# Stick-breaking attention on one core: the running products recorded one step later

## The chip, the core and the metric

The kernel runs on one core of a Trainium2 chip. The metric is the device time of one execution in microseconds (us), the median of several runs of the same program. TensorE (PE in the profile) multiplies matrices, with its weight loads in a row of their own (PEld); VectorE (DVE), ScalarE (ACT) and GpSimd (POOL) work on tiles; SyncE's queue (SP) issues most of the transfers. Each engine takes its instructions in one fixed order, and an instruction starts when the semaphores that it names have come.

## What is computed

A two-layer encoder over 2048 positions of 1024 channels. Layer 0 is a gated pooling mixer, layer 1 is strictly causal stick-breaking attention with 16 heads of 64 channels; each layer ends with a residual and a gated embedding add. The change touches layer 1 alone:

```
q, z = split(rms_norm(x) @ b_w_in);  q = rms_norm(q)       # k, v: once, shared
A[t,s] = beta[t,s] * prod_{s<j<t} (1 - beta[t,j]),  beta = sigmoid(q.k / sqrt(d))
x = x + ((A @ v) * silu(z)) @ b_w_out
x = x + (p[1] @ ple_w[1]) * sigmoid(x @ ple_gate_w[1])
```

The kernel works with the running product of 1 - beta from the newest key backwards. A position's weight is the difference of two neighbouring running products, so the kernel multiplies the products themselves with a v whose rows were differenced beforehand.

## The kernel before

A first part (0 to about 1330 us of the span) computes layer 0 and q, k and v for all four chunks of 512 positions, and stores them. The second part is attention, with the dense work of layer 1 spread between its steps.

**Slots and steps.** A slot is one chunk c of queries, one head h and one chunk kc of keys, from c = 3 down to 0 and within a head from the diagonal chunk (kc = c) back to 0. There are 160 slots. A slot takes four steps, one for each 128 queries (j) and later one for each 128 keys (kt): 640 steps, in the loop at line 1167. One step n does, in the order in which the code is written:

- `turn` (line 943) for the slot that began six steps earlier: up to four 128x128 transposes of running products into a PSUM tile `psa` (L949, PE), the high part of it by a cast (L952, ACT), and the low part by a subtraction on VectorE (L953), called the split here; both go to the tile `at`. There are two `psa` buffers, so the transposes of a step wait for the split two steps earlier.
- `front` (line 917) for the present slot: two matmuls into `psl` (L924, L925, PE), and the sigmoid into one of four tiles `kap` (L928, ACT). It hands back `scan`, the running product on VectorE (L933 on a diagonal slot, L936 elsewhere), which reads `kap` and writes `pp`.
- `scan()`, called at once (line 1184).
- the filler: some passes of dense matmuls from a generator (line 1188; L994, L996 and L998 in `piecewise`). Behind every 24 passes, or 6, a result in PSUM is taken out on VectorE. These three are called the drains here: L1028 in `gate_z` (zr = psd * rb, followed by a sigmoid on ACT, L1032, and a product on POOL, L1033), L1058 in `post` (xr = psd + xr), and L1086 in `post` (sg = psd * sg, followed by an add on POOL, L1087, and one on VectorE, L1088). Each of the four `gate_z` begins with a tile of scales `rb`, of which there is one: four transposes into a `psa` buffer (L1020) and a copy on ACT (L1022), which has to wait until the last L1028 has read the old `rb`.
- `settle` for work put off by some steps, and `gather` (line 956) for the slot that began eight steps earlier: two matmuls of `vv` with `at` (L961, L962, PE).

`shares` (line 1125) sets how many filler passes each step gets while the first chunk of queries runs, out of estimated times of VectorE and TensorE in that step; later the passes are spread evenly.

**What sets the order.** The code's order is a priority. A list scheduler places the instructions engine by engine by its own estimate of when each is ready: an instruction written later goes first where the earlier one is not ready. Instructions marked as kept in program order are not moved. So the order that counts is that of the built program, which is shown in the section on the change. In its rows the running product is named SCALAR_TENSOR_TENSOR, where the profile says TENSOR_TENSOR_SCAN.

Of the kernel before, what the change touches and what calls it, by code (L numbers as in the profile page):

```python
# [35 lines left out]
def trunk_kernel(ctx, tc, x, xt, pt0, wut, cols, heads, zin, grp, aout, agate, aple,  # L36
# [182 lines left out]
    with ExitStack() as st:  # L219
# [41 lines left out]
        def settle():  # L261
            while late:
                late.pop(0)()
# [592 lines left out]
    with ExitStack() as st:  # L856
# [60 lines left out]
        def front(st, j):  # L917

            w = (j + 1) * P if st["diag"] else W5
            r0 = W5 - w  # L920
            ps = psl.tile([P, W5], F32, tag="psl", name="psl")
            qs = slice(j * P, (j + 1) * P)
            (qa, qb), kk = st["q"], st["k"]
            T.matmul(ps[:, :w], qa[:, qs], kk[:, :w], start=True, stop=False)  # L924
            T.matmul(ps[:, :w], qb[:, qs], kk[:, :w], start=False, stop=True)  # L925
            kp = kaps[kcount[0] % NK]
            kcount[0] += 1
            A.activation(out=kp[:, r0:], in_=ps[:, :w], func=AF.Sigmoid, scale=-1.0)  # L928

            def scan():  # L930
                pp = ppool.tile([P, W5], F32, tag="pp", name="pp")
                if st["diag"]:
                    V.tensor_tensor_scan(out=pp[:, r0:][:, ::-1], data0=kp[:, r0:][:, ::-1],  # L933
                                         data1=ahead[:, r0:][:, ::-1], initial=1.0, op0=ALU.mult, op1=ALU.max)
                else:
                    V.tensor_tensor_scan(out=pp[:, ::-1], data0=kp[:, ::-1], data1=zeros.to_broadcast([P, W5]),  # L936
                                         initial=st["carry"][j], op0=ALU.mult, op1=ALU.add)
                st["carry"][j] = pp[:, r0 : r0 + 1]
                st["a"].append((pp, r0))

            return scan

        def turn(st, kt):

            j0 = kt if st["diag"] else 0
            pt = psa.tile([P, W5], F32, tag="psa", name="psa")
            for j in range(j0, 4):
                pp, r0 = st["a"][j]
                T.transpose(pt[:, j * P : (j + 1) * P], pp[:, r0 + kt * P : r0 + (kt + 1) * P], ident)  # L949
            at = t2.tile([P, 2, W5], F32R, tag="at", name="at", bufs=3)  # L950
            cs = slice(j0 * P, W5)
            A.copy(out=at[:, 0, cs], in_=pt[:, cs])  # L952
            V.tensor_tensor(out=at[:, 1, cs], in0=pt[:, cs], in1=f(at[:, 0, cs]), op=ALU.subtract)  # L953
            st["at"][kt] = at

        def gather(st, kt):
            cs = slice((kt if st["diag"] else 0) * P, W5)
            if st["diag"] and kt == 0:
                st["o"].append(pso.tile([P, W5], F32, tag="pso", name="pso"))
            po, at, vv = st["o"][0], st["at"].pop(kt), st["v"]  # L960
            T.matmul(po[:, cs], vv[:, kt, :], at[:, 0, cs], start=(st["diag"] and kt == 0), stop=False)  # L961
            T.matmul(po[:, cs], vv[:, kt, :], at[:, 1, cs], start=False, stop=(st["last"] and kt == 3))  # L962
            if st["last"] and kt == 3:
                half, os, ob, c, h2 = st["h"] % 2, st["os"], st["ob"], st["c"], st["h"] // 2
                mine, other = slice(half * HD, (half + 1) * HD), slice((1 - half) * HD, (2 - half) * HD)

                def gated():
                    zt = t2.tile([P, W5], F32, tag="zt", name="zt", bufs=1)
                    nc.sync.dma_start(out=zt, in_=zd[c][h2])
                    for j in range(4):  # L970
                        js = slice(j * P, (j + 1) * P)
                        stay(A.activation(out=os[:, js], in_=os[:, js], func=AF.Identity,  # L972
                                          bias=ends[c][:, h2, j : j + 1]))
                    G.tensor_tensor(out=os, in0=os, in1=zt, op=ALU.mult)  # L974

                soon(1, lambda: stay(A.copy(out=ob[mine], in_=po[other])))
                soon(2, lambda: stay(A.copy(out=os[mine], in_=po[mine])))
                if half:
                    soon(3, lambda: V.tensor_tensor(out=os, in0=os, in1=ob, op=ALU.add))
                    soon(4, gated)  # L980
                    soon(6, lambda: outs[c].append(os))
# [143 lines left out]
        def shares(n0, n1, total):  # L1125
            scan, turned_, gathered = ([widths(n, lag) for n in range(n0, n1)] for lag in (0, LAG_T, LAG_G))
            vector = [(0.15 + 0.0022 * a if a else 0.0) + (0.14 + 0.00105 * t if t else 0.0) for a, t in zip(scan, turned_)]
            tensor = [2 * max(0.109, 0.2265 * a / W5) * (a > 0) + 0.109 * t / P + 2 * max(0.109, 0.2265 * g / W5) * (g > 0)
                      for a, t, g in zip(scan, turned_, gathered)]
            part = lambda k: [max(0.5, (k * v - t) / 0.2265) + (AHEAD if n0 + i < LAG_T else 0)  # L1130
                              for i, (v, t) in enumerate(zip(vector, tensor))]
            lo, hi = 0.0, 20.0
            for _ in range(60):
                mid = (lo + hi) / 2
                lo, hi = (mid, hi) if sum(part(mid)) < total else (lo, mid)
            return dict(zip(range(n0, n1), part(hi)))
# [12 lines left out]
        for n, (c, _, _) in enumerate(slots):  # L1149
            stops[c] = 4 * (n + 1) + LAG_G + 6  # L1150
        share, even = shares(0, stops[NSUB - 1], NSUB * POSTZ - HELD), 0.0
        done = set()
        ends = {}

        def begin(i):
            c, h, kc = slots[i]
            if kc == c:
                if h == 1:
                    early["ends"] = load_ends(c)
                os = head["os"] if h % 2 else t2.tile([P, W5], F32, tag="os", name="os", bufs=9)  # L1160
                ob = head["ob"] if h % 2 else t2.tile([P, W5], F32, tag="ob", name="ob", bufs=1)
                head.clear()
                head.update(q=early.pop("q", None) or load_q(c, h), carry=[None] * 4, o=[], os=os, ob=ob)
            kk = early["k"].pop(0) if early["k"] else load_k(kc, h)
            active[i] = dict(head, c=c, h=h, k=kk, v=load_v(kc, h), diag=kc == c, last=kc == 0, a=[], at={})

        for n in range(4 * len(slots) + LAG_G):
            now[0] = n
            i2, j2 = divmod(n - LAG_T, 4)
            if 0 <= i2 < len(slots):  # L1170
                turn(active[i2], j2)
            i, j = divmod(n, 4)
            scan = None
            if i < len(slots):
                c, h, kc = slots[i]
                if j == 0:
                    if i == 0:
                        begin(0)
                    if i + 1 < len(slots):
                        begin(i + 1)  # L1180
                scan = front(active[i], j)
                if "ends" in early and j == 2:
                    early.pop("ends")()
            if scan is not None:
                scan()
            owed += even or share.get(n, 0.0)
            while owed >= 1.0:
                next(filler, None)
                owed -= 1.0
            if n >= 4 and n % 4 == 1 and early["s"]:  # L1190
                early["s"].pop(0)()
            if n >= LAG_G and n % 4 == 2 and early["v"]:
                early["v"].pop(0)()
            settle(n)
            i3, j3 = divmod(n - LAG_G, 4)
            if 0 <= i3 < len(slots):
                gather(active[i3], j3)
                if j3 == 3:
                    active.pop(i3)
            for c in range(NSUB - 1, 0, -1):  # L1200
                if len(outs[c]) == 8 and c not in done:
                    done.add(c)
                    for _ in filler:
                        settle()
                    filler = beside(c - 1)
                    if c == NSUB - 1:
                        share = shares(n + 1, stops[c - 1], POST + HELD)
                    else:
                        even = POST / (64.0 * c - (LAG_G + 2 if c == 1 else 1))
                    owed = 0.0  # L1210
# [56 lines left out]
```

## Time and profile before

| | |
|---|---|
| median of 3 runs | 2701.68 us (2701.57 to 2701.96) |
| the profiled execution's own time | 2702.68 us |
| its span, first to last instruction | 2700.8 us |
| DVE busy in the span | 1938.8 us, 72% |
| ACT busy in the span | 1399.2 us, 52% |
| POOL busy in the span | 923.9 us, 34% |
| DMA | 581.56 MB, 215 GB/s on average |

The profile counts an engine as busy from an instruction's start to its end; for PE the ends are modelled, since matmuls are pipelined. A wait is the idle time ahead of an instruction, put down to what ended last before it.

### The profile page before, as it was taken

Reading aid. Unit: us, or ns where it says so; the run is one execution under the profiler, and the core shown is the slowest. Engines: PE = TensorE matmul, PEld = TensorE weight load, DVE = VectorE, ACT = ScalarE, POOL = GpSimd, SP = SyncE. Lnnn points to the kernel's source line nnn. Section 1 sums busy time; section 2 is a strip of 40 time slices with the busy share of each in tenths; the row PEclk is TensorE's granted clock in tenths of the full one; section 3 lists DMA queues with packets and bytes.
Section 4 is the critical chain, followed back from the end, with each engine's and each line's share of the span. In section 5 each row is a group of like instructions: output and inputs, shape, how many; then the busy total and the mean of one; then the engine's idle time right before and its main releaser. Section 6 shows DMA issues by size and latency. Waiting matters only on the chain. (4 is left out here: it accounts for less than half of the span.)

```text
span 2700.8 us, 38620 instructions
## 1 busy us (share of the span) xinstructions
PE 2675.5 (99%) x13352; PEld 2226.3 (82%) x13352; DVE 1938.8 (72%) x2503; ACT 1399.2 (52%) x2735; POOL 923.9 (34%) x725
## 2 busy tenths in 40 slices
PE   9999999999999999999999999999999999999999
PEld 8888888888888888888878888888888888888877
DVE  6776625755367543755399999999999998986632
ACT  6445523455135541445366666666666666665530
POOL 2675338633485425753121111122111211222220
PEclk9999999999999999999999999999999999999999
DMA  8647785567856678444788665555655576668965
GB/s 327 222 169 281 250 302 191 203 228 254 299 173 232 241 243 292 144 150 163 220 237 282 191 209 173 163 169 179 192 161 169 178 215 202 189 199 261 268 220 171
DMA packets 276544, 581.56 MB, mean 215 GB/s; under 512 B 33110, under 2 KB 66902, under 8 KB 276348
## 3 DMA queue, kind: packets, MB, share of 16 engines
q1 hardware_dynamic: 270610, 571.41, 64.6%
q10 hardware_dynamic: 5738, 7.68, 1.0%
q8 instruction: 106, 1.74, 0.3%
q14 instruction: 90, 0.74, 0.1%
HBM read 438.40 MB, written 132.19 MB: 211 GB/s over the span
## 5 line engine op out<-in xcount | busy, mean ns | idle before, releaser
L952 ACT CAST at<-psa 128x512 fp32r<-128x512 f32 (+3 forms) x640 | 334.7, 523 | 436.5 <-PE psa L949 427.1
L614 PE MATMUL psd<-wpair,x 128*128 128x512 f32 x2304 | 536.9, 391 | 0.0
L936 DVE TENSOR_TENSOR_SCAN pp<-kap,pp,zeros 128x512 f32<-128x512 f32 x384 | 513.4, 1337 | 6.3 <-ACT kap L928 5.4
L614 PEld LDWEIGHTS psd<-wpair,x 128*128 128x128 f32 x2304 | 429.9, 188 | 87.1
L953 DVE TENSOR_TENSOR at<-psa,at 128x512 fp32r<-128x512 f32 (+3 forms) x640 | 381.4, 596 | 83.7 <-ACT at L952 78.7
L949 PE MATMUL psa<-ident,pp 128*128 128x128 f32 x2176 | 344.8, 274 | 13.3 <-DVE at L953 12.6
L928 ACT ACTIVATE kap<-psl 128x512 f32<-128x512 f32 (+3 forms) x640 | 345.2, 539 | 13.4 <-PE psl L925 10.5
L949 PEld LDWEIGHTS psa<-ident,pp 128*128 128x128 f32 x2176 | 265.2, 140 | 81.5 <-DVE at L953 26.1
L924 PE MATMUL psl<-kk,qa 128*128 128x512 f32 (+3 forms) x640 | 282.3, 441 | 0.3 <-DMA kk<-kd 0.3
L962 PE MATMUL pso<-at,vv 128*128 128x512 f32 (+3 forms) x640 | 234.4, 366 | 1.2 <-DVE at L953 1.2
L925 PE MATMUL psl<-kk,qb 128*128 128x512 f32 (+3 forms) x640 | 232.9, 364 | 0.0
L961 PE MATMUL pso<-at,vv 128*128 128x512 f32 (+3 forms) x640 | 232.8, 364 | 0.0
L933 DVE TENSOR_TENSOR_SCAN pp<-kap,ahead 128x128 f32<-128x128 f32 (+3 forms) x256 | 227.1, 887 | 5.2 <-ACT kap L928 3.2
L167 PE MATMUL psd<-xp,wpair 128*128 128x512 f32 x512 | 199.6, 390 | 1.4 <-DVE xp L316 1.4
L166 PE MATMUL psd<-xp,wpair 128*128 128x512 f32 x512 | 200.2, 392 | 0.2 <-ACT xp L315 0.2
L168 PE MATMUL psd<-xp,wpair 128*128 128x512 f32 x512 | 199.3, 390 | 0.0
L149 DVE SCALAR_TENSOR_TENSOR wpair<-wraw,gains,wpair 128x512 fp32r<-128x512 f32 x192 | 161.5, 882 | 48.7 <-ACT wpair L148 43.0
L143 POOL TENSOR_TENSOR wpair<-wraw,wpair 128x512 fp32r<-128x512 f32 x99 | 145.4, 1478 | 81.7 <-ACT wpair L141 80.5
L148 ACT ACTIVATE wpair<-wraw,gains 128x512 fp32r<-128x512 f32 x192 | 132.7, 718 | 71.2 <-DMA wraw<-in_bq_dram 32.6
L1033 POOL TENSOR_TENSOR zr<-zr,sgz 128x512 f32<-128x512 f32 x32 | 62.0, 1939 | 309.8 <-ACT sgz L1032 239.8
L141 ACT CAST wpair<-wraw 128x512 fp32r<-128x512 f32 x148 | 90.0, 618 | 121.8 <-PE psd L168 86.6
L962 PEld LDWEIGHTS pso<-at,vv 128*128 128x128 f32 x640 | 120.3, 188 | 27.8 <-DVE at L953 2.0
(196 smaller groups left out, 5364.3 us busy)
## 6 DMA issues: line engine op xcount, KB each, us to landing
kk<-kd SPq DMA_DIRECT2D x320, 128.0 KB
vv<-vd SPq DMA_DIRECT2D x160, 256.0 KB
wraw<-in_kv_dram SPq DMA_DIRECT2D x128, 256.0 KB
wpair<-wzd SPq DMA_DIRECT2D x64, 512.0 KB
wpair<-wod SPq DMA_DIRECT2D x64, 512.0 KB
wpair<-wgd SPq DMA_DIRECT2D x64, 512.0 KB
wpair<-wu SPq DMA_DIRECT2D x48, 512.0 KB
wpair<-wi SPq DMA_DIRECT2D x36, 512.0 KB
```

The source lines that it names most:

```text
L166: T.matmul(ps, wst(units, kt, 0, c0), acts[kt][:, 0], start=(begin and kt == order[0]), stop=False)
L614: T.matmul(pss2[i], ck["x2"][kt][:, xh, tk], wst(ws, kt, wh, 0, W5), start=(kt == 0 and xh == 0 and wh == 0), stop=(kt == KT - 1 and wh == 1))
L924: T.matmul(ps[:, :w], qa[:, qs], kk[:, :w], start=True, stop=False)
L925: T.matmul(ps[:, :w], qb[:, qs], kk[:, :w], start=False, stop=True)
L928: A.activation(out=kp[:, r0:], in_=ps[:, :w], func=AF.Sigmoid, scale=-1.0)
L933: V.tensor_tensor_scan(out=pp[:, r0:][:, ::-1], data0=kp[:, r0:][:, ::-1], data1=ahead[:, r0:][:, ::-1], initial=1.0, op0=ALU.mult, op1=AL ...
L936: V.tensor_tensor_scan(out=pp[:, ::-1], data0=kp[:, ::-1], data1=zeros.to_broadcast([P, W5]), initial=st["carry"][j], op0=ALU.mult, op1=AL ...
L949: T.transpose(pt[:, j * P : (j + 1) * P], pp[:, r0 + kt * P : r0 + (kt + 1) * P], ident)
L952: A.copy(out=at[:, 0, cs], in_=pt[:, cs])
L953: V.tensor_tensor(out=at[:, 1, cs], in0=pt[:, cs], in1=f(at[:, 0, cs]), op=ALU.subtract)
L961: T.matmul(po[:, cs], vv[:, kt, :], at[:, 0, cs], start=(st["diag"] and kt == 0), stop=False)
L962: T.matmul(po[:, cs], vv[:, kt, :], at[:, 1, cs], start=False, stop=(st["last"] and kt == 3))
```

## The change

The call of `scan` is put into a list, and is made at the beginning of the next step, ahead of that step's `turn`.

```
-        done = set()
+        done, behind = set(), []
...
         for n in range(4 * len(slots) + LAG_G):
             now[0] = n
+            if behind:
+                behind.pop()()
             i2, j2 = divmod(n - LAG_T, 4)
             if 0 <= i2 < len(slots):
                 turn(active[i2], j2)
...
             if scan is not None:
-                scan()
+                behind.append(scan)
             owed += even or share.get(n, 0.0)
```

As the code is written, step n's scan then stands behind step n's filler, `settle` and `gather`, and still between the split of step n and that of step n + 1. In the built program PE's order and POOL's are what they were. On VectorE scans and splits alternate as before; of the 96 drains (32 of each kind) 25 change places with the scan ahead of them: 15 L1028, 6 L1058 and 4 L1086. One L1088 goes ahead of a split, two copies L1022 on ACT go ahead of a cast L952, and one cast L1062 on ACT (the high part of a drained xr) ahead of a sigmoid. SP's queue has three changes, each a transfer moved past one neighbour.

The first place is one such swap on VectorE, at the last L1028 of the third `gate_z` (zr is the drained tile, kap and pp belong to the scan, at to the split). Before:

```order
L953 TENSOR_TENSOR at<-psa,at 128x512
L936 SCALAR_TENSOR_TENSOR pp<-kap_12445,pp,zeros 128x512
L953 TENSOR_TENSOR at<-psa,at 128x512
L936 SCALAR_TENSOR_TENSOR pp<-kap_12442,pp,zeros 128x512
L1028 TENSOR_TENSOR zr<-psd,rb 128x512
L953 TENSOR_TENSOR at<-psa,at 128x512
L936 SCALAR_TENSOR_TENSOR pp<-kap_12443,pp,zeros 128x512
```

And of the change, at the same place:

```order
L953 TENSOR_TENSOR at<-psa,at 128x512
L936 SCALAR_TENSOR_TENSOR pp<-kap_12445,pp,zeros 128x512
L953 TENSOR_TENSOR at<-psa,at 128x512
L1028 TENSOR_TENSOR zr<-psd,rb 128x512
L936 SCALAR_TENSOR_TENSOR pp<-kap_12442,pp,zeros 128x512
L953 TENSOR_TENSOR at<-psa,at 128x512
L936 SCALAR_TENSOR_TENSOR pp<-kap_12443,pp,zeros 128x512
```

The drain L1028 and the scan behind the second split have changed places; the splits around them have not moved.

The second place is on ACT, where the third `gate_z` fills `rb` out of `psar`. Before:

```order
L952 CAST at<-psa 128x512
L928 ACTIVATE kap_12444<-psl 128x512
L952 CAST at<-psa 128x512
L1022 COPY rb<-psar 128x512
L928 ACTIVATE kap_12445<-psl 128x512
L1032 ACTIVATE sgz<-zr 128x512
```

And of the change:

```order
L952 CAST at<-psa 128x512
L928 ACTIVATE kap_12444<-psl 128x512
L1022 COPY rb<-psar 128x512
L952 CAST at<-psa 128x512
L928 ACTIVATE kap_12445<-psl 128x512
L1032 ACTIVATE sgz<-zr 128x512
```

The copy L1022 stands one cast earlier. The L1028 that it waits for is one of the 25 that moved.

The third place is on VectorE at the end of the first `post`, with the last drain L1086 there and the add L1088 that waits for POOL's L1087. Before:

```order
L953 TENSOR_TENSOR at<-psa,at 128x512
L936 SCALAR_TENSOR_TENSOR pp<-kap_12443,pp,zeros 128x512
L1086 TENSOR_TENSOR sg<-psd,sg 128x512
L953 TENSOR_TENSOR at<-psa,at 128x512
L1088 TENSOR_TENSOR sg<-sg,x_20497 128x512
L936 SCALAR_TENSOR_TENSOR pp<-kap_12444,pp,zeros 128x512
L953 TENSOR_TENSOR at<-psa,at 128x384
```

And of the change:

```order
L953 TENSOR_TENSOR at<-psa,at 128x512
L1086 TENSOR_TENSOR sg<-psd,sg 128x512
L936 SCALAR_TENSOR_TENSOR pp<-kap_12443,pp,zeros 128x512
L1088 TENSOR_TENSOR sg<-sg,x_20495 128x512
L953 TENSOR_TENSOR at<-psa,at 128x512
L936 SCALAR_TENSOR_TENSOR pp<-kap_12444,pp,zeros 128x512
L953 TENSOR_TENSOR at<-psa,at 128x384
```

The drain L1086 goes ahead of a scan, and the add L1088 ahead of the split behind that scan.

More of the change, by code (lines that the diff above doesn't have):

```diff
@@ L1151, in trunk_kernel @@
         share, even = shares(0, stops[NSUB - 1], NSUB * POSTZ - HELD), 0.0
-        done = set()
+        done, behind = set(), []
         ends = {}
@@ L1168, in trunk_kernel @@
             now[0] = n
+            if behind:
+                behind.pop()()
             i2, j2 = divmod(n - LAG_T, 4)
@@ L1184, in trunk_kernel @@
             if scan is not None:
-                scan()
+                behind.append(scan)
             owed += even or share.get(n, 0.0)
```

## The prediction

> **What bounds the kernel now.** I read the page's table of engines first, then the waits of PE, then stretches of the attention.
>
> ```profile
> span 2700.8 us, 38620 instructions
> PE 2675.5 (99%) x13352; PEld 2226.3 (82%) x13352; DVE 1938.8 (72%) x2503; ACT 1399.2 (52%) x2735; POOL 923.9 (34%) x725
> ```
>
> PE is idle for 2700.8 - 2675.5 = 25.3 us of the whole span. Its order is not changed, so a change that only moves other engines' work can win back at most that, and can cost only by making PE wait.
>
> ```profile
> PE psa L949 <- DVE at L953: 12.6, 21, 1.5
> ...
> PE psl L924 <- DMA kk<-kd: 0.3, 1, 0.3
> ```
>
> ```profile
> DVE at L953 <- ACT at L952: 78.7, 153, 2.2
> ...
> DVE sg L1088 <- POOL sg L1087: 17.1, 12, 2.3
> ```
>
> These are waits, PE's first and then those of all engines: who waited for whom, us in total, how often, the longest. The first is the only place of weight where VectorE holds PE in the attention: the transposes L949 wait for the split L953 that frees their PSUM tile, 21 times in 640 steps. VectorE itself mostly waits for ACT's cast, which follows PE's transposes; so PE leads and VectorE follows.
>
> ```profile
> 1340.00:1900.00 560.00, 553.90 (x3048) 460.12 (x3047) 541.86 (x644) 360.92 (x723) 99.04 (x53) 1.00 0.65 200
> 1900.00:2200.00 300.00, 295.43 (x1642) 247.39 (x1641) 290.81 (x354) 196.59 (x408) 52.18 (x31) 1.00 0.57 177
> ```
>
> Two stretches of the attention: their length, then busy time of PE, PEld, DVE, ACT and POOL, the granted clock (1.00), and the transfers. VectorE is busy for 541.86 / 560 = 97% and 290.81 / 300 = 97%. So it has next to no reserve there: what lengthens its work step after step would soon reach PE. The question is whether a drain in another place does.
>
> **The change part by part.** Nothing is added or removed: 32 drains of each kind, 384 + 256 scans and 640 splits stay. Scans and splits alternate as before. What moves is 25 drains, each from behind a scan to ahead of it.
>
> ```profile
> L1028 DVE TENSOR_TENSOR zr<-psd,rb 128x512 f32<-128x512 f32 x32 | 21.4, 669 | 0.3
> L1086 DVE TENSOR_TENSOR sg<-psd,sg 128x512 f32<-128x512 f32 x24 | 16.2, 675 | 2.5 <-PE psd L998 1.9 <-ACT sg L1082 0.4
> L1058 DVE TENSOR_TENSOR xr<-psd,xr 128x512 f32<-128x512 f32 x24 | 16.2, 673 | 1.1 <-issue 0.8 <-PE psd L998 0.4
> ```
>
> ```profile
> L936 DVE TENSOR_TENSOR_SCAN pp<-kap,pp,zeros x384: 1266/1275/2335, 1341.7 to 2418.9; 128x512 f32<-128x512 f32 x192
> ```
>
> Groups of VectorE from 1340 to 2600 us (busy, mean ns, then idle before), and the scan's least, median and longest duration in ns. A drain takes 0.67 us and waits for nearly nothing; a scan takes 1.28. The ordinary swap is best seen at 1746 us, the first place in the section on the change:
>
> ```profile
> 1744.45 0.40 PE L998 MATMUL psd<-xz,wpair 128*128 128x512 f32 x1
> ...
> 1744.81 0.69 DVE L953 TENSOR_TENSOR at<-psa,at 128x512 fp32r<-128x512 f32 x1
> ...
> 1745.42 1.28 DVE L936 TENSOR_TENSOR_SCAN pp<-kap,pp,zeros 128x512 f32<-128x512 f32 x1
> ...
> 1746.61 0.67 DVE L1028 TENSOR_TENSOR zr<-psd,rb 128x512 f32<-128x512 f32 x1
> ...
> 1747.30 0.69 DVE L953 TENSOR_TENSOR at<-psa,at 128x512 fp32r<-128x512 f32 x1
> ```
>
> Start, duration, engine, line. The dense product ends at 1744.45 + 0.40 = 1744.85, the split at 1745.50. In its new place the drain finds its operand 0.65 us old and starts at once; the scan follows 0.6 us later; the next split starts at 1747.30 as before, since the sum of the two is the same. The drain ends 1.2 us earlier and frees a PSUM tile that PE doesn't ask for until a whole group of passes later, so nothing is gained. The scan ends 0.6 us later; its result is turned at the earliest three steps later, after two more splits and two more scans on VectorE, and its `kap` tile is written again four steps later. That hides it: **0 us**, for 22 of the 25. If VectorE were more than a step behind PE, the cover would be gone, and each would cost 0.6.
>
> In one of the 22 the drain would not start at once:
>
> ```profile
> 1403.48 0.69 DVE L953 TENSOR_TENSOR at<-psa,at 128x512 fp32r<-128x512 f32 x1 [0.23 <-ACT at L952]
> ...
> 1403.90 0.39 PE L998 MATMUL psd<-x,wpair 128*128 128x512 f32 x1
> ...
> 1404.49 1.28 DVE L936 TENSOR_TENSOR_SCAN pp<-kap,pp,zeros 128x512 f32<-128x512 f32 x1 [0.33 <-ACT kap L928]
> ```
>
> Its product ends at 1404.29 and the split at 1404.17, so it waits 0.12, inside the 0.33 that the scan waited for ACT anyway. This too is 0.
>
> SP's three swapped transfers are each a load or store by one neighbour: in the whole attention PE waited 0.3 us for a load of keys, and never longer for one; 0. So with the cast L1062, which stands one sigmoid earlier, and whose result POOL then has sooner: 0.
>
> Three places are different.
>
> **At 1604 us** (the second place in that section) the copy of `rb` waits for the moved drain, and PE waits for the copy:
>
> ```profile
> 1602.32 1.27 DVE L936 TENSOR_TENSOR_SCAN pp<-kap,pp,zeros 128x512 f32<-128x512 f32 x1
> ...
> 1603.14 0.59 ACT L952 CAST at<-psa 128x512 fp32r<-128x512 f32 x1 [1.57 <-PE psa L949]
> 1603.51 0.66 DVE L1028 TENSOR_TENSOR zr<-psd,rb 128x512 f32<-128x512 f32 x1
> 1604.09 0.67 DVE L953 TENSOR_TENSOR at<-psa,at 128x512 fp32r<-128x512 f32 x1
> 1604.20 0.59 ACT L1022 COPY rb<-psar 128x512 f32<-128x512 f32 x1 [0.47 <-DVE zr L1028]
> ...
> 1604.84 0.66 PE L949 MATMUL psa<-ident,pp 128*128 128x128 f32 x4 [0.34 <-ACT rb L1022]
> ```
>
> Now the drain runs from 1602.32 to 1602.98, the copy from about 1603.04 to 1603.63, the cast from 1603.63 instead of 1603.14, and the split from about 1604.24 instead of 1604.09, which nobody on PE asks for at once. The transposes at 1604.84 no longer wait: **-0.34 us**. The other moved copy has no wait of PE behind it: 0.
>
> **At 1782 us** POOL's product lies under a scan:
>
> ```profile
> 1781.62 1.34 POOL L1007 TENSOR_TENSOR og<-os,og 128x512 fp32r<-128x512 f32 x1 [6.15 <-ACT og L1006]
> ...
> 1782.38 1.66 DVE L936 TENSOR_TENSOR_SCAN pp<-kap,pp,zeros 128x512 f32<-128x512 f32 x1
> ...
> 1783.97 0.66 DVE L1028 TENSOR_TENSOR zr<-psd,rb 128x512 f32<-128x512 f32 x1
> 1784.55 0.67 DVE L953 TENSOR_TENSOR at<-psa,at 128x512 fp32r<-128x512 f32 x1
> ...
> 1785.28 0.66 PE L949 MATMUL psa<-ident,pp 128*128 128x128 f32 x4 [1.18 <-DVE at L953]
> ```
>
> The scan takes 1.66 us here and not 1.275, as if it had been held until POOL ended at 1782.96. With the drain first, the scan starts at about 1782.97 and ends well before the transposes that read it, at 1785.28; of all the moved scans this one has the least room. The split comes 1.66 - 1.275 = 0.39 us sooner; PE waits 1.18 for it, so **-0.39 us**. If the length has another cause, it is 0.
>
> [...]
>
> **At 2194 us** (the third place) the add L1088 goes ahead of a split while it waits for POOL:
>
> ```profile
> 2192.40 1.27 DVE L936 TENSOR_TENSOR_SCAN pp<-kap,pp,zeros 128x512 f32<-128x512 f32 x1
> ...
> 2193.59 0.66 DVE L1086 TENSOR_TENSOR sg<-psd,sg 128x512 f32<-128x512 f32 x1
> ...
> 2194.18 0.68 DVE L953 TENSOR_TENSOR at<-psa,at 128x512 fp32r<-128x512 f32 x1
> ...
> 2194.33 1.30 POOL L1087 TENSOR_TENSOR sg<-sg,x 128x512 f32<-128x512 f32 x1 [4.12 <-DVE sg L1086]
> ...
> 2195.65 0.38 PE L949 MATMUL psa<-ident,pp 128*128 128x128 f32 x2
> 2195.67 1.76 DVE L1088 TENSOR_TENSOR sg<-sg,x 128x512 f32<-128x512 f32 x1 [0.82 <-POOL sg L1087]
> ...
> 2199.13 0.33 PE L949 MATMUL psa<-ident,pp 128*128 128x128 f32 x1 [1.46 <-DVE at L953]
> ```
>
> Now L1086 ends at 2193.06, and POOL's L1087 at 2194.43, or at 2195.56 if the scan beside it (to 2194.26) holds it. L1088 then ends at 2196.25 or 2197.4, and the split that PE needs at 2195.65 ends at 2196.85 or 2198.0: a new wait of 1.2 to 2.3 us. In return VectorE is through before PE comes to the transposes at 2199.13, whose 1.46 go. PE's work between the two transposes is 2199.13 - 1.46 - 2195.65 = 2.02, so they start at about 2198.9 or 2200.0 instead of 2199.13, and the next wait shifts likewise. I bound the place by -0.6 and +0.9 and take **0**, which lies between.
>
> The sum is -0.34 - 0.39 + 0 = -0.73. Against the profiled execution's own 2702.68 us that gives 2701.95; it ran 1.00 us above the median, and the median becomes 2701.68 - 0.73 = **2701.0 us**.
>
> **The rivals.**
>
> *Faster: the drains' earlier end lets VectorE keep ahead, and PE's waits for the split go.* Worth 12.6 us at most, 2689 us. For it speaks that those waits sit where VectorE was late; against it that the swaps leave VectorE's sum alone, and that only the few places above lie within 3 us of such a wait.
>
> *Slower: a drain at the head of VectorE's queue waits for its dense product, and scan and split wait behind it.* Before, a scan covered that wait. Places: the 25 swaps. It decides once PE's last pass ends later than the split ahead of the drain, 0.65 us later than at 1744 us. If PE ran a step later against VectorE (1.8 us from split to split there), each swap would cost 1.8 - 0.65 = 1.15, and all 25 on PE's path 29 us: 2730. Against it: where VectorE is the late one, that many steps don't tip over; a few would give 2703 to 2709.
>
> *Slower, by POOL:* L1028 and L1086 feed POOL, whose products start 1.2 us earlier and may now start ahead of a scan. L1088 shows what such a hold can be (least, median and longest, in ns):
>
> ```profile
> L1088 DVE TENSOR_TENSOR sg<-sg,x x32: 658/692/1764, 2045.5 to 2696.9; 128x512 f32<-128x512 f32 x32
> ```
>
> The longest is 1.07 us above the median. 19 such drains by 1.07 are 20 us of VectorE; 21 of 640 splits hold PE, so 0.7 us would reach it, 2702; all of it only if VectorE had no reserve, 2721. [...]
>
> *The change does less than it says:* it does, since scans keep their place among the splits in all 640 steps; that is in the sum already.
>
> **How the numbers follow.** 0.2% is 5.4 us, about what a measurement of this kernel can tell from no change: below 2696.3 is faster, above 2707.1 slower. Forecast 0.80, PE's waits gone 0.06, drains that wait 0.08, POOL's hold 0.06. Half of the first rival's chance stays within 0.2%, and about a third of the other two's: faster 0.03, same 0.88, slower 0.09. The range goes down by the waits of PE near swaps that could go in full (0.79 left at 1785, 1.46 at 2199), and by some 1.8 for others that shift: 2697. Upwards it takes the 0.9 and the 0.39 of the places above, POOL's 0.7, and two new waits of 1.46: about 2706.
>
> **What would show it.** In the profile after: PE's idle time within 5 us of 25.3; its waits for L953 still around 12.6; no wait of L1028, L1058 or L1086 for L998 beyond those above; no 0.34 at the third L1022; a shorter scan near 1782; a changed pair of waits near 2196 and 2199. A drain that waits on PE, or many scans above 1.28 us, would make it wrong.

## The result, and the profile after

| | before | after |
|---|---|---|
| median, timed side by side (22 runs each) | 2701.85 us (2700.82 to 2703.85) | 2705.08 us (2702.86 to 2708.39) |
| ratio after to before | | 1.0012, 95% interval 1.0007 to 1.0018 |
| the profiled execution's own time | 2702.68 us | 2706.99 us |

The change costs 3.2 us, 0.12%. The forecast was a gain of 0.73. The time is inside the range and within 0.2%, as the largest chance had it, but the sign was wrong, and it shows beyond the interval.

The page after, its span and its busy times:

```profile
span 2705.1 us, 38622 instructions
PE 2678.1 (99%) x13352; PEld 2227.0 (82%) x13352; DVE 1945.1 (72%) x2503; ACT 1398.7 (52%) x2735; POOL 914.0 (34%) x725
```

The counts are those of before. VectorE is busy for 1945.1 - 1938.8 = 6.3 us longer with the same 2503 instructions, and POOL for 923.9 - 914.0 = 9.9 us less with the same 725. Both are only busy with the same work in another order, so busy time has changed hands. PE's idle time went from 25.3 to 2705.1 - 2678.1 = 27.0.

The groups that hold most of it, by line (busy, mean ns | idle before). Before:

```profile
L936 DVE TENSOR_TENSOR_SCAN pp<-kap,pp,zeros 128x512 f32<-128x512 f32 x384 | 513.4, 1337 | 6.3 <-ACT kap L928 5.4
L933 DVE TENSOR_TENSOR_SCAN pp<-kap,ahead 128x128 f32<-128x128 f32 (+3 forms) x256 | 227.1, 887 | 5.2 <-ACT kap L928 3.2 <-POOL ahead L871 0.9
L1033 POOL TENSOR_TENSOR zr<-zr,sgz 128x512 f32<-128x512 f32 x32 | 62.0, 1939 | 309.8 <-ACT sgz L1032 239.8 <-issue 24.6 <-DMA pin<-in_pt_dram 18.5
```

After:

```profile
L936 DVE TENSOR_TENSOR_SCAN pp<-kap,pp,zeros 128x512 f32<-128x512 f32 x384 | 519.3, 1352 | 4.5 <-ACT kap L928 3.6
L933 DVE TENSOR_TENSOR_SCAN pp<-kap,ahead 128x128 f32<-128x128 f32 (+3 forms) x256 | 228.9, 894 | 5.1 <-ACT kap L928 3.2 <-POOL ahead L871 0.9
L1033 POOL TENSOR_TENSOR zr<-zr,sgz 128x512 f32<-128x512 f32 x32 | 55.1, 1723 | 313.6 <-ACT sgz L1032 260.4 <-issue 23.5 <-DVE at L953 17.1
```

The scans take 5.9 + 1.8 = 7.7 us more, POOL's product L1033 6.9 us less. Of the 384 full-width scans 16 take over 2 us, where 8 did before.

PE's waits after:

```profile
PE psa L949 <- DVE at L953: 13.6, 24, 2.0
```

The wait for the split grew by 1.0 us, and the 0.3 for `rb` is not there.

**Where it is lost.** PE's order is the same, so the start of L924 in each of the 640 steps can be laid beside that of before. The first part of the program, whose code is the same, ended 1.61 us later in this execution; in the four other profiles used below it ended between 0.47 us earlier and 1.08 later, so that is the execution and not the change. In the attention the difference doesn't grow evenly. It jumps at a few steps, listed with the experiments below.

The typical loss, at an L1028 of the fourth `gate_z`. VectorE and POOL before (start, duration):

```profile
1801.86 1.27 DVE L936 TENSOR_TENSOR_SCAN pp<-kap,pp,zeros 128x512 f32<-128x512 f32 x1
1803.05 0.67 DVE L1028 TENSOR_TENSOR zr<-psd,rb 128x512 f32<-128x512 f32 x1
...
1802.30 1.93 POOL L1007 TENSOR_TENSOR og<-os,og 128x512 fp32r<-128x512 f32 x1 [15.65 <-ACT og L1006]
1804.46 2.12 POOL L1033 TENSOR_TENSOR zr<-zr,sgz 128x512 f32<-128x512 f32 x1 [0.23 <-PE psa L949]
```

And after:

```profile
1802.98 0.68 DVE L1028 TENSOR_TENSOR zr<-psd,rb 128x512 f32<-128x512 f32 x1
1803.58 2.22 DVE L936 TENSOR_TENSOR_SCAN pp<-kap,pp,zeros 128x512 f32<-128x512 f32 x1
...
1815.00 0.66 DVE L953 TENSOR_TENSOR at<-psa,at 128x512 fp32r<-128x512 f32 x1
...
1803.43 1.29 POOL L1007 TENSOR_TENSOR og<-os,og 128x512 fp32r<-128x512 f32 x1 [16.61 <-ACT og L1006]
...
1815.71 0.66 PE L949 MATMUL psa<-ident,pp 128*128 128x128 f32 x4
```

POOL's L1007 depends on ACT and on nothing that moved. Before, it became ready under a scan; it took 1.93 us where it takes 1.29 after, and the scan 1.27. After, the drain stands at that moment on VectorE, which takes 0.68 on both sides; POOL starts 0.15 us ahead of the scan, and the scan takes 2.22. The one that starts second takes longer here: before it was POOL (1.93 against 1.29), which has time, and after it is VectorE (2.22 against 1.27), which has none. VectorE is now 2.22 - 1.27 = 0.95 us late. It keeps that lag through the next five splits, since it has no idle time there, and PE meets it at the next diagonal slot, where the matmuls are short (L924 takes 0.30 us at 128 columns there, 0.47 at 512 in the step before): the sixth split starts at 1815.00 and ends at 1815.66, and the transposes start at 1815.71. A table by stretch shows the missing reserve (length, PE, PEld, DVE, ACT, POOL, clock, transfers):

```profile
1803.00:1815.70 12.70, 12.65 (x74) 10.43 (x72) 12.70 (x15) 7.94 (x16) 2.69 (x2) 1.00 0.65 197
```

VectorE is busy for 12.70 of 12.70 us.

Laid beside each other one by one, the scans show this at eleven places (steps 46, 94, 124, 183, 250, 260, 278, 369, 380, 403 and 526; the one of 403 is an L933 of full width, the others are L936): the scan there took 1.22 to 1.28 us before and takes 2.14 to 2.30 after. They are of two kinds. At six of them (250, 260, 278, 380, 403 and 526) the held scan is the moved one, and L1007 starts ahead of it, as above. At the other five it is the scan behind the moved one, and what starts ahead of it is a POOL instruction that the moved drain feeds: L1033 at 46, 94, 124 and 183, L1063 at 369. Against the start of the same step's L924 it comes 0.3 to 0.6 us sooner than before. Step 46, before:

```profile
1422.97 0.66 DVE L1028 TENSOR_TENSOR zr<-psd,rb 128x512 f32<-128x512 f32 x1
...
1424.15 1.27 DVE L936 TENSOR_TENSOR_SCAN pp<-kap,pp,zeros 128x512 f32<-128x512 f32 x1
...
1424.37 2.13 POOL L1033 TENSOR_TENSOR zr<-zr,sgz 128x512 f32<-128x512 f32 x1 [4.18 <-DMA xz<-x2p]
```

And after:

```profile
1422.74 0.68 DVE L1028 TENSOR_TENSOR zr<-psd,rb 128x512 f32<-128x512 f32 x1
1423.34 1.27 DVE L936 TENSOR_TENSOR_SCAN pp<-kap,pp,zeros 128x512 f32<-128x512 f32 x1
...
1425.11 2.17 DVE L936 TENSOR_TENSOR_SCAN pp<-kap,pp,zeros 128x512 f32<-128x512 f32 x1
...
1424.90 1.29 POOL L1033 TENSOR_TENSOR zr<-zr,sgz 128x512 f32<-128x512 f32 x1 [3.75 <-DMA xz<-x2p]
```

Before, L1033 came 0.22 us behind the scan of that step and took 2.13; after, it comes 0.21 us ahead of it, and the scan takes 2.17.

At seven of the eleven some of the loss comes back at once, since the next scan was held before (1.66 to 2.33 us) and now is less or not. What is left, 0.3 to 1.5 us, is VectorE's lag. Behind eight of the eleven PE's start jumps within 3 to 11 steps; behind the other three (183, 260 and 369) the lag is gone before PE asks.

**The third place.** VectorE, POOL and PE after:

```profile
2195.32 0.68 DVE L1086 TENSOR_TENSOR sg<-psd,sg 128x512 f32<-128x512 f32 x1
2195.92 1.27 DVE L936 TENSOR_TENSOR_SCAN pp<-kap,pp,zeros 128x512 f32<-128x512 f32 x1
2198.32 1.74 DVE L1088 TENSOR_TENSOR sg<-sg,x 128x512 f32<-128x512 f32 x1 [1.13 <-POOL sg L1087]
2199.99 0.68 DVE L953 TENSOR_TENSOR at<-psa,at 128x512 fp32r<-128x512 f32 x1
...
2196.07 2.21 POOL L1087 TENSOR_TENSOR sg<-sg,x 128x512 f32<-128x512 f32 x1 [2.94 <-DVE sg L1086]
...
2200.72 0.44 PE L949 MATMUL psa<-ident,pp 128*128 128x128 f32 x2 [2.00 <-DVE at L953]
...
2201.72 0.40 PE L998 MATMUL psd<-og,wpair 128*128 128x512 f32 x1
2201.95 0.60 PE L994 MATMUL psd<-og,wpair 128*128 128x512 f32 x1
2202.35 0.63 PE L961 MATMUL pso<-at,vv 128*128 128x512 f32 x1
2202.77 0.63 PE L962 MATMUL pso<-at,vv 128*128 128x512 f32 x1
```

Here the scan is first, and L1087 takes 2.21 us where it took 1.30 before; L1088 waits for it, the split waits for L1088, and PE waits 2.00 us for the split. That is the later of the prediction's two cases. Then comes something that it did not have: from 2201.95 the passes follow each other by 0.40 and 0.42 us instead of 0.23. The windows show why (columns as above; pieces of 3.41 us, cut where the recorded clock changes):

```profile
2198.56:2201.97 3.41, 1.41 (x9) 1.12 (x9) 3.41 (x4) 0.75 (x3) 0.96 (x1) 1.00 0.50 193
2201.97:2205.39 3.42, 3.42 (x11) 2.75 (x10) 3.42 (x7) 1.50 (x4) 0.00 (x0) 0.50 0.82 235
2205.39:2208.80 3.41, 3.41 (x22) 3.08 (x22) 1.69 (x3) 1.59 (x4) 0.00 (x0) 1.00 0.87 288
```

The granted clock was 0.50 from 2201.97 to 2205.39, and 1.00 around it. The place costs 1.40 us in this execution.

### The profile page after: what moved, and what is told of

The parts are those of the page before. It is cut to its first block, busy times and chain, and to the rows that moved or that the text cites. A ratio compares the mean times of both kernels' runs of the same rounds, so it can differ in the third digit from the quotient of the medians.

```text
span 2705.1 us, 38622 instructions
## 1 busy us (share of the span) xinstructions
PE 2678.1 (99%) x13352; PEld 2227.0 (82%) x13352; DVE 1945.1 (72%) x2503; ACT 1398.7 (52%) x2735; POOL 914.0 (34%) x725
## 4 chain that ended last, share of the span: by engine, by line
PE 85%; DVE 8%; issue 3%; DMA 2%; ACT 1%; POOL 1%; SPq 0%; ACTq 0%; DVEq 0%; POOLq 0%
PE psd L614 19%; PE psd L166 9%; PE psd L167 9%; PE psd L168 9%; PE psa L949 7%; PE psd L994 5%; PE psd L996 5%; PE psd L998 5%; DVE pp L936 4%; PE psl L925 3%; PE pso L962 3%; PE psl L924 3%; PE pso L961 3%; DVE at L953 2%; PE pst L719 1%
## 5 line engine op out<-in xcount | busy, mean ns | idle before, releaser
L952 ACT CAST at<-psa 128x512 fp32r<-128x512 f32 (+3 forms) x640 | 334.8, 523 | 443.8 <-PE psa L949 434.0
L936 DVE TENSOR_TENSOR_SCAN pp<-kap,pp,zeros 128x512 f32<-128x512 f32 x384 | 519.3, 1352 | 4.5 <-ACT kap L928 3.6
L949 PE MATMUL psa<-ident,pp 128*128 128x128 f32 x2176 | 345.3, 274 | 13.9 <-DVE at L953 13.6
L924 PE MATMUL psl<-kk,qa 128*128 128x512 f32 (+3 forms) x640 | 282.5, 441 | 0.0
L933 DVE TENSOR_TENSOR_SCAN pp<-kap,ahead 128x128 f32<-128x128 f32 (+3 forms) x256 | 228.9, 894 | 5.1 <-ACT kap L928 3.2
L1033 POOL TENSOR_TENSOR zr<-zr,sgz 128x512 f32<-128x512 f32 x32 | 55.1, 1723 | 313.6 <-ACT sgz L1032 260.4
```

## The experiments

Two theories. **The hold:** the loss comes from POOL's instructions that now start ahead of a scan. **The late scan:** the swap itself makes scans and splits late, by a drain's 0.6 us, and VectorE is too busy to make it up; POOL only happens to be there. Both say that the loss is at the swapped places, so the first four kernels ask for that, and the next four for POOL.

**Parts of the change.** Each of the four takes the change and defers the scan only in some steps. The edit is one line; this one is for the steps before the first `post`:

```
-                behind.append(scan)
+                (behind.append if n < 292 else lambda fn: fn())(scan)
```

*The `gate_z` places alone* (n < 292; the 15 L1028 move):

> The scan is put off only in steps below 292, where the filler is gate_z: the 15 moved L1028 stay moved, the L1058, L1086 and L1088 stand as before. Theory H (a moved drain lets POOL's product start ahead of a scan and the scan is held for up to 0.95 us; the lag reaches PE at the next diagonal slot): by the profile of the change the steps to 292 come out at +0.5 us (losses of about 0.3 to 0.55 at 1430, 1519, 1815 and 1859, gains of 0.55, 0.56 and 0.39 at 1405, 1605 and 1786), so 2702.4. Theory L (each swap costs alike, because each scan is 0.6 us later): 15/25 of +3.2, so 2703.8. Theory N (nothing of it lies in the attention): 2701.9 or 2705.1 by chance of the build, and no new waits at those places.

*The `post` places alone* (n >= 292):

> The scan is put off only from step 292 on, where the filler is post: 6 L1058, 4 L1086 and the one L1088 moved, the 15 L1028 as before. H: by the profile of the change this stretch comes out at +2.2 to +2.7 us, 1.4 of it at the add L1088 near 2199, so 2704.1 to 2704.6. L: 10/25 of +3.2, so 2703.1. N: as for the first.

*All but the third place* (not 458 <= n < 466):

> The change without the third place: in steps 458 to 465 the scan is issued at once, so the L1086 and the L1088 near 2199 stand as before and the other 24 drains stay moved. H: the new wait of 2.00 us at the transposes near 2200, and the stretch of lower granted clock behind it, go back to 1.46 and 0.48 at full clock: 1.4 us less than the change, 2703.7. L: 24/25 of +3.2, so 2705.0. If the half clock in 2200 to 2210 comes from something other than PE's idle time there, it shows here again.

*The three steps with a gain, or thought free* (n in 36, 142, 239):

> The scan is put off in steps 36, 142 and 239 alone: three L1028 (near 1405, 1603 and 1784) and the copy of rb near 1604 move, nothing else. H: the gains of the change without its losses, 0.55 + 0.56 + 0.39 = 1.5 us below the kernel before: 2700.3. L: three swaps cost 3/25 of 3.2, so 2702.2. N: 2701.9.

The jumps of PE against before, in us, from the starts of L924 in the profiled executions, where they are over 0.2 and the change makes them; and the medians of 11 runs against the 2702.25 us of before on the same chip (for the whole change, the figures of the result). Two rows below them hold four smaller jumps that go with the swaps as well, and a pair that cancels:

| step, start before (us) | after | gate_z alone | post alone | without third | three steps |
|---|---|---|---|---|---|
| 50, 1428.62 | +0.37 | +0.37 | | +0.38 | |
| 97, 1517.45 | +0.36 | +0.37 | | +0.37 | |
| 144, 1605.25 (`rb`) | -0.56 | -0.57 | | -0.55 | -0.57 |
| 242, 1785.69 (shorter scan) | -0.39 | -0.38 | | -0.39 | -0.39 |
| 258, 1814.72 | +0.29 | +0.28 | | +0.29 | |
| 282, 1858.72 | +0.55 | +0.55 | | +0.55 | |
| 384, 2046.99 | +0.33 | | +0.30 | +0.31 | |
| 414, 2102.50 | +0.23 | | +0.22 | +0.23 | |
| 464 to 466, 2195.79 (third place) | +1.40 | | +0.31 | | |
| 530, 2325.87 | +0.32 | | +0.32 | +0.32 | |
| 49, 130, 281 and 407 | +0.65 | +0.50 | +0.17 | +0.64 | |
| 89 and 90, +0.38 and -0.42 | -0.03 | -0.03 | | -0.03 | |
| sum | +3.52 | +1.09 | +1.32 | +2.12 | -0.96 |
| median | | 2703.58 | 2703.43 | 2704.26 | 2701.49 |
| against before | +3.23 | +1.33 | +1.18 | +2.01 | -0.76 |
| ratio, 95% interval | 1.0012 (1.0007 to 1.0018) | 1.0003 (0.9994 to 1.0012) | 1.0003 (0.9994 to 1.0012) | 1.0006 (0.9998 to 1.0015) | 0.9995 (0.9986 to 1.0004) |

Left out are jumps that don't go with the swaps. One of -0.24 at 2449 is in all five profiles. One of -0.54 to -0.55 at 1403 is in four of them, that of the `post` kernel too, which makes no swap there, while the kernel of three steps, which makes it, shows -0.17: it is the wait for a load of keys in the one execution of before. The others stand in single profiles; the largest is the first kernel's -1.59 at 1498 to 1500.

Every jump of the table is there to within 0.03 us in each kernel that has its swap, and in none that has not; only the third place varies. So the places add up, and next to none of the loss is spread over the other steps. The medians follow the sums to within 0.3 us, though the interval of each of the four holds 1.

Against the expectations the medians alone would not have decided. 2703.58, 2703.43 and 2701.49 lie nearer to what the late scan forecast (2703.8, 2703.1, 2702.2) than to the hold's figures (2702.4, 2704.1 to 2704.6, 2700.3); only 2704.26 lies nearer to the hold's 2703.7 than to 2705.0. The hold's figures had been misread off the profile: they counted the -0.55 at 1403 as a gain of the swap there, left out the smaller jumps, and put the dip of the clock into the `post` kernel. What speaks against the late scan is where the jumps are. After the change all 25 moved scans start 0.5 to 0.7 us later against PE's step than before. PE loses behind nine of them: eight with a held scan, and the third place. Two gain. Behind the other 14 it loses nothing over 0.05 that lasts, though VectorE has no idle time in the 6 us behind nine of these.

The last kernel keeps what the change gains and none of what it loses; its median is 0.76 below before, which by its interval isn't certain. It was the version to keep, if any.

At the third place the `post` kernel shows what is left without the dip of the clock. PE, with its wait:

```profile
2197.90 0.44 PE L949 MATMUL psa<-ident,pp 128*128 128x128 f32 x2 [1.98 <-DVE at L953]
...
2199.12 0.40 PE L994 MATMUL psd<-og,wpair 128*128 128x512 f32 x1
2199.36 0.39 PE L961 MATMUL pso<-at,vv 128*128 128x512 f32 x1
...
2201.65 0.66 PE L949 MATMUL psa<-ident,pp 128*128 128x128 f32 x4 [0.28 <-DVE at L953]
```

The wait is as long, 1.98, but the passes follow by 0.24, and the place costs 0.31. In the profile of after it cost 1.40, so the dip was worth about 1.1 us there.

**Without POOL's reads.** Before and the change, each without the attention's POOL instructions that read SBUF (four L690 of the first part, which run on to about 1360 us, stay). The products L1033 and L974 and POOL's additions L1087 are left out, and the low parts L1007 and L1063 are set to zero, which POOL does without reading (0.53 us each):

```
-                    G.tensor_tensor(out=os, in0=os, in1=zt, op=ALU.mult)
+                    pass
...
-                    G.tensor_tensor(out=zr, in0=zr, in1=sg, op=ALU.mult)
...
-                    G.tensor_tensor(out=pr[:, 1], in0=xr, in1=f(pr[:, 0]), op=ALU.subtract)
+                    G.memset(f(pr[:, 1]), 0.0)
```

The same 25 drains move between the two, and two L1088 beside them. Before, without the reads:

> The kernel before with no GpSimd instruction that reads SBUF in the attention: the product L1033 is left out (the sigmoid alone is stored as the gate), the gate's product L974 and the add L1087 are left out, and the low halves that L1007 and L1063 make are set to zero by a memset. It is the base for the next run. H (a scan is held while a GpSimd instruction reads SBUF): every scan L936 takes 1.27 to 1.30 us and none 1.6 or more (a memset only writes), VectorE's busy time falls by some 30 us, and PE's waits for the split by most of 12.6: 2690 to 2697. If the long scans come from something else, they stay, and the time with them.

The change, without the reads:

> The change, with the same work left out. H: with nothing on GpSimd that could hold a scan, the 25 swaps cost nothing: against the run before it, -0.6 us (the copy of rb, 0.56; near 1784 and 2199 nothing is left to win or lose) to +0.3, and no jumps in the steps behind the moved drains. L (a scan that starts 0.6 us later costs by itself): the jumps stay, +2 us or more against the run before it.

Medians of 5 runs 2682.38 (2681.91 to 2683.25) and 2681.82 (2681.31 to 2683.89), against 2702.17 for before on that chip. Page, groups and PE's waits of the first:

```profile
PE 2669.3 (100%) x13352; PEld 2229.4 (83%) x13352; DVE 1901.8 (71%) x2503; ACT 1398.1 (52%) x2735; POOL 711.2 (27%) x637
...
L936 DVE TENSOR_TENSOR_SCAN pp<-kap,pp,zeros 128x512 f32<-128x512 f32 x384 | 491.2, 1279 | 8.8 <-ACT kap L928 7.7
```

And groups, waits and one swapped place of the second:

```profile
L936 DVE TENSOR_TENSOR_SCAN pp<-kap,pp,zeros 128x512 f32<-128x512 f32 x384 | 490.7, 1278 | 7.9 <-ACT kap L928 6.7
...
PE psa L949 <- DVE at L953: 1.3, 3, 0.8
...
1794.29 0.69 DVE L953 TENSOR_TENSOR at<-psa,at 128x512 fp32r<-128x512 f32 x1 [0.19 <-ACT at L952]
1794.90 0.68 DVE L1028 TENSOR_TENSOR zr<-psd,rb 128x512 f32<-128x512 f32 x1
1795.50 1.28 DVE L936 TENSOR_TENSOR_SCAN pp<-kap,pp,zeros 128x512 f32<-128x512 f32 x1
1796.69 0.67 DVE L953 TENSOR_TENSOR at<-psa,at 128x512 fp32r<-128x512 f32 x1
```

Of the 384 scans 382 take 1.29 us or less in both. The two longer ones (2.07 and 1.70 us in the first kernel, 1.61 and 1.70 in the second) each lie beside one of the L690 that are left. The swapped drain and scan take 0.68 and 1.28, and the swaps cost 2681.82 - 2682.38 = -0.56 us, nothing that can be told from zero, where they cost 3.2 with the reads. PE's wait for the split falls from 12.6 to 1.3 us in both kernels. PE's starts differ by more than 0.2 us at two places: -0.37 at step 17, behind the first of those held scans, and +0.71 at 97 and 98, where VectorE is late because a load came late (L1070 waited 0.88 for ACT, and ACT for the load). At the other places of the table nothing is lost. The late scan, which had every swap cost as before, does not fit: the same swaps are there, and PE does not meet them. The first kernel is also faster than the 2690 to 2697 expected, so the reads cost more than was thought. One limit: the omission also gives VectorE reserve, by some 37 us (1938.8 - 1901.8), and takes away L1088's wait for POOL. So this alone doesn't tell a missing hold from a late scan that is forgiven; the next pair leaves all the work in.

**POOL's instructions in pieces.** All of them stay, each cut into four of 128 columns, so that by the hold a scan that is second would wait for a shorter one:

```
+        def pooled(out, in0, in1, op):
+            w = W5 // 4
+            for i in range(4):
+                cs = slice(i * w, (i + 1) * w)
+                G.tensor_tensor(out=out[:, cs], in0=in0[:, cs], in1=in1[:, cs], op=op)
...
-                    G.tensor_tensor(out=os, in0=os, in1=zt, op=ALU.mult)
+                    pooled(out=os, in0=os, in1=zt, op=ALU.mult)
```

and so for the other four. Before in pieces:

> The kernel before with each of GpSimd's five kinds of 128x512 instructions in the attention (L974, L1007, L1033, L1063, L1087) cut into four of 128x128. H: a scan is held for one piece (0.35 us or so) and not for 1.3, so no scan takes 2.2 us, L936 sums to less than 513 us, and PE's wait for the split falls below 12.6: 2697 to 2701. Rival: the pieces' own overhead and their waits for scans make L1088 wait longer for L1087 (17.1 us now), and nothing is won: 2702 to 2705.

The change in pieces:

> The change with the same cut. H: the 25 swaps cost less than 1 us against the run before it, since a hold is a quarter as long. L: they cost the same 2 to 3 us. If it is H and the cut helps at all, 2697 to 2701, below both kernels.

Medians of 11 runs 2702.93 (ratio to before 1.0001, 0.9992 to 1.0010) and 2701.55 (0.9996, 0.9987 to 1.0005). Both lie above the 2697 to 2701 that the hold had for them. Cut up, the change's median lies 1.4 us below that of its own before, where uncut it lay 3.2 above. The scans of the first (L942 is L936 there; least, median and longest in ns), and VectorE's wait for POOL:

```profile
L942 DVE TENSOR_TENSOR_SCAN pp<-kap,pp,zeros x384: 1262/1274/1666, 1342.8 to 2420.0; 128x512 f32<-128x512 f32 x192
...
DVE sg L1094 <- POOL sg L902: 37.6, 23, 3.1
```

The longest scan is 1.67 us, where it was 2.33 before (it lies beside an L690, which isn't cut; beside a piece the longest is 1.59). The waits for the split went to 11.1 us, but the add (L1094 here, L1088 before) now waits 37.6 us for POOL instead of 17.1, so the cut itself gains nothing, as the rival had it. Between the pair the swaps no longer lengthen the scans at all (497.2 us in the first, 496.8 in the second). How much of their cost is gone isn't settled by the medians, which say all of it, with intervals of some 2.4 us on either side of each. The profiles say that PE loses about 0.9 us in the attention, against 3.5 uncut (2.4 without the dip of the clock), if one wait of the first kernel is left aside, which the change did not touch:

```profile
1406.09 0.47 PE L930 MATMUL psl<-kk,qa 128*128 128x512 f32 x1 [1.13 <-DMA kk<-kd]
```

At the five places in the `gate_z` (steps 49 and 50, 97, 130, 258, 281 and 282) nothing over 0.01 us is lost, where uncut it was 0.2 to 0.7 each; in the 6 us behind those moved scans VectorE is busy for 96% or more. The late scan would have cost as much cut as uncut, since the drains moved by as much. At 384, 407 and 530, in the `post`, +0.37, +0.37 and +0.28 are left. At 384 POOL's four pieces of L1007 take 3.56 us, in the first kernel 2.28, and the add L1094 waits 1.96 us for POOL, in the first kernel 1.54.

## Why the prediction failed, step by step

- **The ordinary swaps, "That hides it: 0 us, for 22 of the 25": wrong, and this is the step that failed.** The argument followed the operands: dense product, split, scan, and who reads them. That much held: behind 14 of the 25 swaps the late scan costs nothing, and without POOL's reads it costs nothing anywhere. It did not follow POOL. At six places L1007 becomes ready at the same moment as before and now meets a drain instead of a scan, and at five the POOL instruction that the moved drain feeds comes sooner; either way POOL starts ahead of a scan, which then takes 2.14 to 2.30 us. Eight of these places cost PE 3.1 us in all (2.45 in the table's jumps over 0.2, 0.65 in the smaller ones).
- **The rival "Slower, by POOL" had the mechanism, and priced it wrongly twice.** It took products fed by a moved drain; L1007, which no moved drain feeds, does it as well, and makes 2.0 of the 3.1 us. It took 19 holds of 1.07, 20 us of VectorE; the scans grew by 7.7. And it let "21 of 640 splits" of it reach PE, 0.7 us. About 3.1 of 7.7 did, two fifths. The share of steps in which PE waits is the wrong factor: VectorE was 97% busy, and behind eight of the eleven long scans its lag was not forgiven in the steps where nobody waited, but carried to the next step where PE did, 3 to 11 steps on. With these two numbers the rival would have stood at 2704 instead of 2702, and with more than a chance of 0.06.
- **At 1604, -0.34: right in kind, measured -0.56.** The wait for `rb` is gone, and the jump is larger than the wait that was shown; why was not followed up.
- **At 1782, -0.39: right to 0.01.** The wait is 0.79 after, as worked out:

```profile
1786.39 0.66 PE L949 MATMUL psa<-ident,pp 128*128 128x128 f32 x4 [0.79 <-DVE at L953]
```

  In the sum, the row of the profile, a scan of 1.66 us that started under a POOL instruction, was applied to the one place where it gave a gain. The same at eight other places, where a scan now starts under a POOL instruction, was the loss. The traces of before and after have it throughout: the 57 and 63 of the 384 L936 that took over 1.29 us all started while a POOL instruction ran, and none of those that started ahead of one, or beside none, took more. The drain L1028 was not lengthened: all 32 took 0.66 to 0.69 us in both, also the four of before that started under a POOL instruction. And POOL's zeroing, which reads nothing, lengthened no scan (the 28 and 25 scans that ran beside one in the two kernels took 1.29 us or less). Why the one waits for the other, no trace shows.
- **The third place, -0.6 to +0.9, taken as 0:** +0.31 without the dip, which is inside; +1.40 with it, which is not. The wait was the longer of the two cases (2.00, forecast 1.2 to 2.3).
- **"A drain at the head of VectorE's queue waits for its dense product": didn't happen.** After, as before, L1086 waited 1.9 us in all for L998, L1058 less, and L1028 not.
- **"PE's waits for the split go": they grew**, 12.6 to 13.6, and how much of them hung on POOL was not seen: without POOL's reads 1.3 were left.

## What to carry to other kernels

When an instruction is moved, look at what runs on the other engine at that moment, not only at the operands: where two engines hold each other off (here a scan took 2.22 us instead of 1.27, or a POOL instruction 1.93 instead of 1.29), a swap on one of them changes who starts first, and with it who pays. On an engine with next to no reserve (VectorE, 97% busy here) a delay isn't to be multiplied by the share of steps in which somebody waits; follow it to the next step in which somebody does. And a change whose parts add up, place by place, can be kept in parts: three of the swaps, two of which gain, come out 0.76 us below before (not certain by the interval), the whole change 3.2 above.

## What was not expected of the hardware

- **The clock after a short wait.** PE was idle for 2.00 us at 2200, and its granted clock was 0.50 for 3.41 us behind it; with an idle time of 1.98 at that place in the `post` kernel, and 1.46 before, it stayed at 1.00. At 2.00 against 1.98 the length of the one wait hardly tells the first two apart. In the stretch of 3.41 us just ahead of the dip PE was busy for 1.41, or 41%, shown at the third place. Where the clock could change is an estimate from its recorded lengths: after, the full clock lasted 2194.77 us ahead of the dip, the dip 3.413, and the full clock behind it 498.35; before, the full clock lasted 2693.12 without a dip. These are 643, 1, 146 and 789 times 3.41333, to 0.01 us. Laid out in pieces of that length, from where the full clock begins in its own trace, the wait of the `post` kernel falls across a border:

```profile
2193.48:2196.88 3.40, 2.45 (x13) 1.65 (x11) 2.28 (x2) 1.57 (x3) 3.22 (x2) 1.00 0.90 338
2196.89:2200.30 3.41, 2.40 (x14) 2.10 (x15) 3.41 (x5) 1.31 (x4) 0.00 (x0) 1.00 0.58 180
```

  PE was busy for 2.45 and 2.40 us of the two, 72% and 70%, and the clock stayed at 1.00. Laid out alike, the piece with most of the 1.46 of before has 2.24 us, 66%. A piece at the very end of the kernel before has 1.62 us, 47%, and the full clock behind it as well. So what the clock follows is not shown; no run tried it directly. The medians of the first two parts come to 1.33 + 1.18 = 2.51 us, the whole change to 3.23; a dip in many of its runs would make up for that, but the intervals are too wide to show it.
- **What POOL's reads cost the whole kernel.** Leaving them out took 19.8 us off before, with 22.2 us less in the full-width scans alone (513.4 to 491.2) and PE's idle time down from 25.3 to 2681.5 - 2669.3 = 12.2 us; the rest is in PE's busy time, whose ends are modelled. Where that work could go instead wasn't tried.
